# Attention with short convolution on one core: first maxima taken later, bank-freeing products ahead of splits, and load buffers of its own for the last y

## The chip, the core and the metric

The kernel runs on one core of a Trainium2 chip. A core has TensorE (PE: matmuls, with PEld for the loading of their stationary operand), VectorE (DVE), ScalarE (ACT), GpSimd (POOL) and SyncE (SP, which here only issues DMAs). Each engine runs its own list of instructions in order; they wait for one another by semaphores. PE writes only into PSUM, whose banks hold 128 x 512 numbers of 32 bits; DVE and ACT read it out. The metric is the device time of one execution in microseconds (us).

## What is computed

One layer of a diffusion backbone, batch 1, 1024 latent tokens on a grid of 16 x 64, 256 context tokens, model width 1024:

```python
h = rmsnorm(x, norm_g) * (1 + scale[:, None]) + shift[:, None]
hc = rmsnorm(ctx, norm_g) * (1 + scale_c) + shift_c
q, k, v, za, u, bg, cg, zc = jnp.split(h @ w_in, SPLIT_POINTS, axis=-1)
...
attn = neighbourhood_attention(q, k, heads(v), kc, vc, rpb) * jax.nn.silu(za)
conv = gated_short_conv(u, bg, cg, zc, conv_w, conv_b)
x_new = x + gate[:, None] * (jnp.concatenate([attn, conv], axis=-1) @ w_out)
```

The attention has 8 heads of 64. A query sees a window of 8 x 16 latent keys with a learned position bias, and all context keys, in one softmax. The convolution branch is `bg * conv3(cg * u) * silu(zc)` over 512 channels.

## The kernel before

Every product is made of three matmuls: each operand is split into a rounded high part (a cast on ACT) and the rest (a subtraction on DVE), and high x high, high x low and low x high are summed in PSUM (`mm3`). So each block of weights costs a load, a cast and a "split" before PE can use it.

There are three stages. In the first the inputs are normed, and q, k, v are projected and spilled to HBM. The second is the attention, in which all four engines run in an order written out by hand: every instruction is chained behind the one before it on its engine (`strict`). The third is the output projection, where the planner that builds the kernel orders the instructions of each engine itself, by when it believes that their inputs are there.

**The attention** runs over 35 quarters (`quarter(n)`, L1123), one fourth of a head each, as a software pipeline. Quarter n makes the scores of unit n (two key blocks against the queries that see them), the context scores of unit n+1, the exponentials of unit e = n-2, and the products with v of unit o = n-3. Keys lie along partitions, so the maximum over the keys of a query is a maximum over partitions. It goes this way: running maxima are kept in `mx` (DVE, `ctx_max` and `lat_max`); PE turns a block of 128 queries of it into a bank `pmx` (a transpose); DVE reduces it to one column `rm`; PE turns that column back, spread over all partitions; ACT copies it to `mg`, and DVE subtracts `mg` from the scores ahead of the exponential. `turned(e)` gives the blocks that are needed for unit e: one for e = -1 and for the last, two for the others.

Before the change all of this stands at the head of a quarter: turn and reduction first, then the products of the context (`ctx_out`) and waiting DVE work, then the turn back and the copy, then the scores. In quarter 1 (e = -1) and quarter 2 (e = 0) there are no products yet between turn and turn back.

**Filler.** Between the steps of a quarter PE works at 16 "units", the projections of the gates and of the convolution branch: each is a [1024 x 128] slice of `w_in` against h in two halves of 512 tokens, each half in one of two PSUM banks (`pu`, tag "U", L369). One call of `next(fill)` is a tick of six matmuls. `TICKS[n]` says how many ticks quarter n has. The work of the other engines for the filler is put in queues of "chores": `soon` (splits of the next unit's weights, copies, the product `cu`) and `slow` (convolution taps and products `cv`). `do_dves(3)` in a quarter emits up to three DVE chores, `soon` first. A chore with `frees` set (L469) is the product `times(half, ps, True)` of a unit CBG, which reads the unit's bank; the next unit's half may not start before it.

**The output stage** needs y[f] for eight blocks f, in the order 4, 5, 6, 0, 1, 2, 3, 7 (`FORDER`). `put_y` (L1417) loads a half into `tb`, casts it to `yh` on ACT and subtracts on DVE to give `yl`. Blocks 0 to 3 are the pairs of attention heads, 4 to 7 the convolution groups. Pair 3 is finished here: its gate `zs` and its sums `rb` are loaded too. All `tb` and `zs` come from one ring of four buffers (tag "zt"); the loads are issued from ACT's queue. `yh` and `yl` of the last block lie in the pool `rp`, which takes over the space of h once the last unit is through.

Of the kernel before, what the change touches and what calls it, by code (L numbers as in the profile page):

```python
# [10 lines left out]
F32 = mybir.dt.float32  # L11
# [3 lines left out]
ALU = mybir.AluOpType  # L15
AX = mybir.AxisListType
# [3 lines left out]
P = 128  # L20
# [6 lines left out]
NH, HD = 8, 64  # L27
# [2 lines left out]
CTXT = 3  # L30
FORDER = [4, 5, 6, 0, 1, 2, 3, 7]

TICKS = [2, 3, 3, 3, 3, 2, 3, 3, 2] + 2 * (8 * [3] + 2 * [4]) + 3 * [3] + [4, 5, 4]
EPS = 1e-6


# [3 lines left out]
def body(tc, es, x, ctxt, w_ada, b_ada, w_in, q_g, k_g, rpbr, w_out, vecs, cst, out):  # L40
# [21 lines left out]
    pe, act, dve, pool = every = [ordered(e) for e in (nc.tensor, nc.scalar, nc.vector, nc.gpsimd)]  # L62
    sp = ordered(nc.sync)

    def sbuf(name, side=None, bufs=1):
        kw = {} if side is None else {"side": side}
        return tc.tile_pool(name=name, bufs=bufs, reuse_waits="tile", **kw)

    def psum(name):
        return tc.tile_pool(name=name, bufs=1, space=PSUM, reuse_waits="tile")  # L70
# [42 lines left out]
    ident = ci[:, 0:P]  # L113
# [207 lines left out]
    def do_acts():  # L321
        for c in soon + (slow if not any(c[1] and c[1].__name__ == "product" for c in soon) else []):
            if c[0]:
                c[0]()
                c[0] = None

    def do_dves(most=99):
        for queue in chores:
            while queue and not queue[0][0] and (queue is soon or most > 0 and not soon):
                on_dve = queue.pop(0)[1]  # L330
                if on_dve:
                    on_dve()
                    most -= 1
# [45 lines left out]
    def blocked(v):  # L379
        return v.rearrange("p (b r c) -> p b r c", b=2, r=16)  # L380

    def by_row(v):
        return v.rearrange("p (r b c) -> p b r c", r=16, b=2)

    def natural(v, half):
        return v.rearrange("p (r b c) -> p b r c", r=16, b=4)[:, 2 * half:2 * half + 2]
# [136 lines left out]
    def load_sums(f, half, rb, queue):  # L523
        for i in range(2):
            queue.dma_start(rb[64 * i:64 * i + 64],
                            ri_d[f][i:i + 1, half * 512:(half + 1) * 512].broadcast_to([64, 512]))
# [306 lines left out]
    for m in range(1, 4):  # L833
        k, new, last = 2 * m, m < 3, m == 3
# [84 lines left out]
    psm = es.enter_context(psum("psm"))  # L919
# [182 lines left out]
    def pair_of(n):  # L1102

        h, g = divmod(n, 4)
        return [(a, heads[h], 2 * g + a) for a in range(2)] if 0 <= h < NH else []

    def both(v, n, part=slice(0, 31)):

        lo, hi = span(2 * (n % 4))
        return v[:, :, part.start * 12:min(part.stop, hi - lo) * 12]  # L1110

    def maxima_of(n):

        lo, hi = span(2 * (n % 4))
        v = mg[:]
        return bass.AP(v.tensor, v.offset + lo * 16, [list(v.ap)[0], [4, 2], [16, hi - lo], [1, 12]])

    def turned(n):

        g = n % 4  # L1120
        return [b for b, there in (((2 * g + 2) % NB, n + 1 < 4 * NH), (2 * g + 1, n >= 0)) if there][::-1 if g < 3 else 1]

    def quarter(n):  # L1123

        live = lambda m: 0 <= m < 4 * NH
        ticks = TICKS[n]
        e, o = n - 2, n - 3  # L1130
        blocks = turned(e) if -1 <= e < 4 * NH else []
        nb = len(blocks)
        if blocks:
            pm = psm.tile([P, 512], F32, name="pmx", tag="C", bufs=2)
            for i, b in enumerate(blocks):
                pe.transpose(pm[:, i * P:(i + 1) * P], mx[:, b * P:(b + 1) * P], ident)
            rm = ap.tile([P, 2], F32, name="rm", tag="rm", bufs=8)
            dve.tensor_reduce(rm[:, :nb], pm[:, :nb * P].rearrange("p (i k) -> p i k", i=nb), AX.X, ALU.max)
        while lat_rest:
            lat_rest.pop()()  # L1140
        if live(o):
            heads[o // 4].ctx_out(o % 4)
        do_dves(3)
        if gating and next(gating[0], "end"):
            gating.pop(0)
        if blocks:
            for i in range(nb):
                pe.transpose(pm[:, 256 + i * P:256 + (i + 1) * P], rm[:, i:i + 1].broadcast_to([P, P]), ident)
            v, step = mg[:, blocks[0] * P:], (blocks[-1] - blocks[0]) * P or P
            act.copy(bass.AP(v.tensor, v.offset, [list(v.ap)[0], [step, nb], [1, P]]),  # L1150
                     pm[:, 256:256 + nb * P].rearrange("p (i k) -> p i k", i=nb))
        now = pair_of(n)
        for i, hd_, j in now:
            hd_.scores(j, sbank[:, i])
        if n == 0:
            next(fill)
            ticks -= 1
        ctx_now = [m for m in ([0, 1] if n == 0 else [n + 1]) if live(m)]
        for m in ctx_now:
            heads[m // 4].ctx_scores(m % 4)  # L1160
        if live(e):
            ctx_rest = heads[e // 4].ctx_exp(e % 4)
            sb = sbs.pop(e)
            w = both(sb, e)
            w4 = w.rearrange("p a (c r) -> p a c r", r=12)
            dve.tensor_tensor(w4, w4, maxima_of(e), ALU.subtract)
            exps[e] = [ap.tile([P, 2, 384], F32R, name=m, tag=m, bufs=2) for m in ("phl", "pll")]
            ph, pl = (both(v, e) for v in exps[e])
            act.activation(ph, w, AF.Exp)
            act.activation(w, w, AF.Exp)  # L1170
        for _ in range(n > 0):
            next(fill, None)
        done = []
        if o >= 0:
            pho, plo = exps.pop(o)
            for i, hd_, j in pair_of(o):
                hd_.lat_out(j, pho[:, i], plo[:, i])
                if j in (5, 7):
                    done.append((hd_, j // 7))
                    if j == 7 and hd_.s:  # L1180
                        ready.append(hd_.p)
        if now:
            sb = sbs[n] = sb_new()
            bt = now[0][1].bt[:].rearrange("p v n -> p (v n)")[:, :1128].rearrange("p (a n) -> p a n", a=2)
            for at, slot, w_ in (((0, 31, 8), (8, 15, 16)), ((0, 0, 31),), ((0, 0, 31),), ((0, 0, 15), (15, 39, 8)))[n % 4]:
                dve.tensor_tensor(sb[:, :, at * 12:(at + w_) * 12], sbank[:, :, at * 12:(at + w_) * 12],
                                  bt[:, :, slot * 12:(slot + w_) * 12], ALU.add)
            for m in ctx_now:
                heads[m // 4].ctx_max(m % 4)
            for i, hd_, j in now:  # L1190
                hd_.lat_max(j, sb[:, i])
        if live(e):
            ctx_rest()
            lat_rest.append(lambda: dve.tensor_tensor(pl, w, ph.bitcast(F32), ALU.subtract))
            if n + 1 >= len(TICKS) or TICKS[n + 1] == 2:
                lat_rest.pop()()
        for _ in range(ticks - (n > 0)):
            next(fill, None)
        for hd_, bank_ in done:
            hd_.finish(bank_)  # L1200
        do_acts()
# [36 lines left out]
    for n in range(NT + 3):  # L1238


        p, t = divmod(n, NB)
# [122 lines left out]
    with sbuf("att") as ap, psum("psb") as psb:  # L1364
        sbank = psb.tile([P, 2, 512], F32, name="pss")
        strict[:] = every
        mx = ap.tile([P, T], F32, name="mx")
        sb_new = lambda: ap.tile([P, 2, 384], F32, name="sb", tag="sb", bufs=3)
        mg = ap.tile([P, T], F32, name="mg")
        heads[0].load_v()  # L1370
        for n in range(len(TICKS)):
            h, g = divmod(n, 4)
# [7 lines left out]
            if ready:  # L1380
                p = ready.pop()
# [20 lines left out]
    op = es.enter_context(sbuf("op"))  # L1402
# [14 lines left out]
    def put_y(yp, f):  # L1417

        yh = yp.tile([P, T], F32R, name=f"yh{f}")
        yl = yp.tile([P, T], F32R, name=f"yl{f}")  # L1420
        for half in range(2):
            cols = slice(half * 512, (half + 1) * 512)
            tb = op.tile([P, 512], F32, name="tb", tag="zt", bufs=4)
            if f == NPAIR - 1:
                zs = op.tile([P, 512], F32, name="zs", tag="zt", bufs=4)
                rb = op.tile([P, 512], F32, name="rb", tag="rb", bufs=2)
                act.dma_start(zs, z_d[f][:, cols])
                act.dma_start(tb, o_d[f][:, cols])
                load_sums(f, half, rb, pool)
                act.activation(zs, zs, AF.Silu)  # L1430
                dve.tensor_tensor(zs, zs, rb, ALU.mult)
                dve.tensor_tensor(tb, tb, zs, ALU.mult)
            else:
                act.dma_start(tb, y_d[f][:, cols])
            tv = blocked(tb[:]) if f < NPAIR else by_row(tb[:])
            act.copy(natural(yh[:], half), tv)  # L1436
            dve.tensor_tensor(natural(yl[:], half), tv, natural(yh[:].bitcast(F32), half), ALU.subtract)
        y[f] = yh, yl
# [93 lines left out]
```

## Time and profile before

| | us |
|---|---|
| median of 3 runs | 633.08 |
| runs | 632.79 to 636.38 |
| the profiled execution | 633.06 |
| its span, from first to last instruction | 631.3 |
| granted TensorE clock, mean | 1.000 |

Of the span the projections take until about 266 us (the first scores follow), the attention with its filler until about 522, the last convolution unit until 539, and the output projection the rest. Times of instructions in the profile are from the start of the span. In a row of the timeline stand start, length, engine, line, operation, output <- inputs, sizes, and how many instructions were merged; in brackets the idle time of the engine before it and what ended it. Operations that go through the ordering helper all have its line, L55, so they are told apart by their tiles. "ACTq" and "SPq" are DMA issues from the queues of ACT and SP. The columns of a stretch (rows "a:b") are its length, the busy time of PE, PEld, DVE, ACT and POOL, the granted clock, the share of the DMA engines' time and GB/s.

### The profile page before, as it was taken

Reading aid. Unit: us, or ns where it says so; the run is one execution under the profiler, and the core shown is the slowest. Engines: PE = TensorE matmul, PEld = TensorE weight load, DVE = VectorE, ACT = ScalarE, POOL = GpSimd, SP = SyncE. Lnnn points to the kernel's source line nnn. Section 1 sums busy time; section 2 is a strip of 40 time slices with the busy share of each in tenths; the row PEclk is TensorE's granted clock in tenths of the full one; section 3 lists DMA queues with packets and bytes.
Section 4 is the critical chain, followed back from the end, with each engine's and each line's share of the span. In section 5 each row is a group of like instructions: output and inputs, shape, how many; then the busy total and the mean of one; then the engine's idle time right before and its main releaser. Section 6 shows DMA issues by size and latency. Waiting matters only on the chain.

```text
span 631.3 us, 10013 instructions
## 1 busy us (share of the span) xinstructions
PE 622.9 (99%) x3488; PEld 538.6 (85%) x3488; DVE 433.5 (69%) x889; ACT 326.7 (52%) x712; POOL 78.6 (12%) x102
## 2 busy tenths in 40 slices
PE   8999999999999999989999999999999999999998
PEld 3577899999999999878888888888888888878887
DVE  1887857866857755467897778987998865585111
ACT  4776935425626446346576568567774845450000
POOL 1305014123223222000000000000000002004100
PEclk9999999999999999999999999999999999999999
DMA  8983638967875993975475562766542235964521
GB/s 315 363 290 109 179 122 263 280 207 221 273 247 176 293 335 134 338 230 213 135 237 150 181 194 104 239 232 193 171 135 76 60 109 148 359 208 149 197 101 50
DMA packets 104030, 126.45 MB, mean 200 GB/s; under 512 B 10689, under 2 KB 70553, under 8 KB 102700
## 3 DMA queue, kind: packets, MB, share of 16 engines
q1 hardware_dynamic: 97516, 114.24, 54.7%
q10 hardware_dynamic: 6208, 11.05, 5.5%
q0 software_dynamic: 256, 0.54, 0.3%
q8 instruction: 27, 0.44, 0.3%
q14 instruction: 23, 0.19, 0.1%
HBM read 89.04 MB, written 39.04 MB: 203 GB/s over the span
## 4 chain that ended last, share of the span: by engine, by line
PE 89%; DMA 4%; DVE 3%; issue 1%; ACT 1%; POOL 0%; SPq 0%; ACTq 0%; DVEq 0%; POOLq 0%
PE pu L55 27%; PE pacc L55 21%; PE po L55 8%; PE acc L55 6%; PE tr L55 5%; PE cacc L55 4%; PE pout L74 3%; PE pout L76 3%; PE pout L75 3%; PE pss L55 3%; PE pmx L55 2%; PE pc L55 2%; DMA tb<-y_d 2%; DMA woraw<-in_w_out 2%; PE trA L55 1%
## 5 line engine op out<-in xcount | busy, mean ns | idle before, releaser
L55 PE MATMUL pu<-h,uh 128*128 128x512 f32 x544 | 169.7, 393 | 0.9 <-DVE cv L55 0.9
L55 PE MATMUL pacc<-w,h 128*128 128x384 f32 x768 | 138.4, 337 | 0.0
L55 PEld LDWEIGHTS pacc<-w,h 128*128 128x128 f32 x768 | 132.8, 188 | 0.2
L55 PEld LDWEIGHTS pu<-h,uh 128*128 128x128 f32 x544 | 97.6, 188 | 18.0 <-DVE cv L55 1.3
L55 PE MATMUL pu<-h,ul 128*128 128x512 f32 x272 | 106.5, 392 | 0.0
L55 PEld LDWEIGHTS pu<-h,ul 128*128 128x128 f32 x272 | 51.1, 188 | 11.1
L55 POOL TENSOR_TENSOR ss<-ss,few 128x4 f32<-128x4 f32 (+1 forms) x40 | 42.0, 1050 | 124.7 <-DVE ss L55 124.7
L74 PE MATMUL pout<-woh,yh 128*128 128x512 f32 (+2 forms) x136 | 51.6, 380 | 0.3 <-ACT yh L1436 0.3
L75 PE MATMUL pout<-wol,yh 128*128 128x512 f32 (+2 forms) x136 | 51.6, 379 | 0.0
L76 PE MATMUL pout<-woh,yl 128*128 128x512 f32 (+2 forms) x136 | 50.8, 379 | 0.0
L55 PE MATMUL acc<-h,w 128*128 128x512 f32 x144 | 38.1, 404 | 0.8 <-ACT h L55 0.8
L55 ACT ACTIVATE sq<-pacc 128x256 f32<-128x256 f32 x32 | 12.4, 387 | 48.2 <-PE pacc L55 44.3
L55 DVE TENSOR_REDUCE rm<-pmx 128x2 f32<-128x256 f32 (+1 forms) x33 | 13.7, 416 | 33.8 <-PE pmx L55 33.7
L55 ACT COPY mg<-pmx 128x256 f32<-128x256 f32 (+1 forms) x33 | 12.1, 366 | 47.1 <-PE pmx L55 37.7
L55 DVE TENSOR_TENSOR mx<-mx,sb 128x372 f32<-128x372 f32 (+2 forms) x64 | 31.8, 498 | 2.0
L55 PE MATMUL po<-phl,v 128*65 128x276 f32 (+2 forms) x192 | 32.0, 269 | 0.0
L55 ACT ACTIVATE qn<-pacc,ss 128x64 f32<-128x64 f32 x128 | 30.2, 332 | 3.0 <-POOL ss L55 3.0
L55 DVE TENSOR_REDUCE ss<-sq 128x4 f32<-128x260 f32 (+1 forms) x40 | 15.6, 391 | 22.9 <-ACT sq L55 22.9
L55 PEld LDWEIGHTS acc<-h,w 128*128 128x128 f32 x144 | 25.5, 188 | 6.5 <-ACT h L55 1.2
L1462 DVE TENSOR_TENSOR ot<-pout,xr 128x512 f32<-128x512 f32 (+2 forms) x9 | 5.7, 632 | 36.5 <-PE pout L76 36.5
L74 PEld LDWEIGHTS pout<-woh,yh 128*128 128x128 f32 x136 | 25.6, 188 | 5.4 <-ACT yh L1436 0.7
L76 PEld LDWEIGHTS pout<-woh,yl 128*128 128x128 f32 x136 | 25.6, 188 | 4.7
(159 smaller groups left out, 1188.8 us busy)
## 6 DMA issues: line engine op xcount, KB each, us to landing
uraw<-in_w_in SPq DMA_DIRECT2D x34, 256.0 KB
q_d<-qs SPq DMA_DIRECT2D x32, 256.0 KB
k_s<-k_d SPq DMA_DIRECT2D x8, 1024.0 KB
q_s<-q_d SPq DMA_DIRECT2D x16, 512.0 KB
wr<-in_w_in SPq DMA_DIRECT2D x40, 192.0 KB
slab<-in_w_ada SPq DMA_DIRECT2D x6, 1024.0 KB
v_d<-vs SPq DMA_DIRECT2D x20, 260.0 KB
v<-v_d SPq DMA_DIRECT2D x16, 325.0 KB
```

The lines of the kernel that those rows point to most:

```text
L55: i = emit(*a, **kw)
L74: i = pe.matmul(ps, ah, bh, start=first, stop=False)
L75: pe.matmul(ps, ah, bl, start=False, stop=False)
L76: pe.matmul(ps, al, bh, start=False, stop=last)
L1462: dve.tensor_tensor(ot[:, c], ps[c.start][:, c], xr[:, c], ALU.add)
```

## The change

Four edits. (1) The maxima become a function in two steps. For e = -1 the turn and reduction move from the head of quarter 1 to behind its scores, its maxima on DVE and its first tick, and the turn back with its copy to behind the quarter's other ticks. For e = 0 the turn stays at the head of quarter 2, and the turn back moves behind the scores and context scores. From e = 1 on nothing moves. (2) `do_dves` first takes a chore that frees a bank, if one stands at the head of `slow`. (3) The last three quarters have 5, 4, 4 ticks instead of 4, 5, 4. (4) The loads of the last y get two buffers in its own pool.

```diff
-TICKS = [2, 3, 3, 3, 3, 2, 3, 3, 2] + 2 * (8 * [3] + 2 * [4]) + 3 * [3] + [4, 5, 4]
+TICKS = [2, 3, 3, 3, 3, 2, 3, 3, 2] + 2 * (8 * [3] + 2 * [4]) + 3 * [3] + [5, 4, 4]
...
     def do_dves(most=99):
+        while most > 0 and slow and slow[0][2] is not None and not slow[0][0]:
+            slow.pop(0)[1]()
+            most -= 1
         for queue in chores:
...
+    def maxima(e):
+
+        blocks = turned(e) if e < 4 * NH else []
+        nb = len(blocks)
+        if not blocks:
+            return None
+        pm = psm.tile([P, 512], F32, name="pmx", tag="C", bufs=2)
+        for i, b in enumerate(blocks):
+            pe.transpose(pm[:, i * P:(i + 1) * P], mx[:, b * P:(b + 1) * P], ident)
+        rm = ap.tile([P, 2], F32, name="rm", tag="rm", bufs=8)
+        dve.tensor_reduce(rm[:, :nb], pm[:, :nb * P].rearrange("p (i k) -> p i k", i=nb), AX.X, ALU.max)
+
+        def back():
+            for i in range(nb):
+                pe.transpose(pm[:, 256 + i * P:256 + (i + 1) * P], rm[:, i:i + 1].broadcast_to([P, P]), ident)
+            v, step = mg[:, blocks[0] * P:], (blocks[-1] - blocks[0]) * P or P
+            act.copy(bass.AP(v.tensor, v.offset, [list(v.ap)[0], [step, nb], [1, P]]),
+                     pm[:, 256:256 + nb * P].rearrange("p (i k) -> p i k", i=nb))
+        return back
...
     def quarter(n):
...
+        back = maxima(e) if e >= 0 else None
...
+        if back and n > 2:
+            back()
         now = pair_of(n)
         for i, hd_, j in now:
             hd_.scores(j, sbank[:, i])
...
             heads[m // 4].ctx_scores(m % 4)
+        if back and n == 2:
+            back()
         if live(e):
...
             for i, hd_, j in now:
                 hd_.lat_max(j, sb[:, i])
+        back = maxima(-1) if n == 1 else None
         if live(e):
...
         for _ in range(ticks - (n > 0)):
             next(fill, None)
+        if back:
+            back()
         for hd_, bank_ in done:
...
-            tb = op.tile([P, 512], F32, name="tb", tag="zt", bufs=4)
+            tb = yp.tile([P, 512], F32, name="tb", tag="zt", bufs=4 if yp is op else 2)
```

The lines taken out of `quarter` (turn, reduction, turn back and copy at its head) are those of the new function.

More of the change, by code (lines that the diff above doesn't have):

```diff
@@ L1130, in quarter @@
         e, o = n - 2, n - 3
[L1131 to L1138, printed above, removed]
+        back = maxima(e) if e >= 0 else None
         while lat_rest:
@@ L1145, in quarter @@
             gating.pop(0)
[L1146 to L1151, printed above, removed]
+        if back and n > 2:
+            back()
         now = pair_of(n)
```

## The prediction

> **What bounds the kernel now.** I read the page first, then the list of waits of TensorE, then the timeline around each of those waits.
>
> ```profile
> span 631.3 us, 10013 instructions
> ## 1 busy us (share of the span) xinstructions
> PE 622.9 (99%) x3488; PEld 538.6 (85%) x3488; DVE 433.5 (69%) x889; ACT 326.7 (52%) x712; POOL 78.6 (12%) x102
> ```
>
> TensorE (PE) is busy 99% of the span, and the change neither adds nor drops a matmul. So a gain can only come out of the time in which PE stands still, and a loss only out of new standstills. These are two of PE's waits that the change aims at (total, times, longest); a third, on `mx`, and one at the end stand in the timelines further down:
>
> ```profile
> PE pu L55 <- DVE cv L55: 0.9, 2, 0.5
> PE pmx L55 <- DVE rm L55: 0.9, 2, 0.5
> ```
>
> A wait costs more than its idle time, because the ends of matmuls are modelled and overlap the next start. I therefore measure by starts. The chain of waits has stretches without a gap that give the steady steps (start, length, instructions):
>
> ```profile
> 274.47 4.09 PE pu L55 x18
> ...
> 482.51 1.63 PE pu L55 x6
> ...
> 509.97 0.11 PE pmx L55
> ```
>
> A filler matmul of 512 columns takes 4.09/18 = 0.227 us; a "tick" of filler (six of them) is 1.36, three ticks are 4.09. A turn (`pmx`, one block) takes 0.11.
>
> **The first maxima (1.5 us gained).** PE at the start of the attention, quarters 1 and 2 (start, length, instruction):
>
> ```profile
> 271.08 0.39 PE L55 MATMUL pu<-h,ul 128*128 128x512 f32 x1
> 272.31 0.30 PE L55 MATMUL pmx<-ci,mx 128*128 128x128 f32 x1 [0.84 <-DVE mx L55]
> 272.99 0.32 PE L55 MATMUL pmx<-ci,rm 128*128 128x128 f32 x1 [0.38 <-DVE rm L55]
> 273.07 0.93 PE L55 MATMUL pss<-q_s,k_s 128*128 128x372 f32 x4
> 273.83 0.63 PE L55 MATMUL pc<-q_s,kc_s 128*128 128x256 f32 x4
> ...
> 278.40 0.38 PE L55 MATMUL pmx<-ci,mx 128*128 128x128 f32 x2
> 279.29 0.43 PE L55 MATMUL pmx<-ci,rm 128*128 128x128 f32 x2 [0.52 <-DVE rm L55]
> ```
>
> The last filler matmul starts at 271.08 and leaves PE free at 271.31; the turn of the maxima starts at 272.31: 1.00 lost. The turn back could start 0.11 later, at 272.42, and starts at 272.99: 0.57 lost. In quarter 2 two turns take 0.22, and the turn back starts 0.89 after the first of them: 0.67 lost. Together 2.24 us.
>
> With the change quarter 1 goes straight to the scores (273.07 to 273.83: 0.76), the context scores (from 273.83 to three ticks before quarter 2's start at 278.40, that is 274.31: 0.48) and a tick. Then come the turn, two ticks and the turn back. Scores start at 271.31, so the turn is due at 271.31 + 0.76 + 0.48 + 1.36 = 273.91, and the turn back 0.11 + 2.73 later, at 276.75. Nothing may be late there:
>
> ```profile
> 271.21 0.95 DVE L55 TENSOR_TENSOR mx<-mx,sb 128x288 f32<-128x288 f32 x2
> ...
> 275.58 1.12 DVE L55 TENSOR_TENSOR mx<-mx,sb 128x372 f32<-128x372 f32 x2
> ...
> 280.17 0.69 DVE L55 TENSOR_TENSOR sc<-sc,mg 128x512 f32<-128x512 f32 x1 [0.33 <-ACT mg L55]
> ...
> 282.74 1.13 DVE L55 TENSOR_TENSOR mx<-mx,sb 128x372 f32<-128x372 f32 x2
> ```
>
> The first quarter's maxima are done at 271.21 + 0.95 = 272.16, well before 273.91. The second quarter's end 3.63 after its scores begin (273.07 to 276.70), so at 274.94. The reduction stands behind them on VectorE (DVE) and has until 276.75. Both stalls of quarter 1 are hidden.
>
> Quarter 2 then begins at 276.86 and puts scores and context scores (1.24) between the turn (0.22) and the turn back, which falls at 278.32. The reduction's round trip of 0.89 ends at 277.75, so this stall is hidden too. The transposes and context scores share a ring of two banks, whose order shifts by one: quarter 2's context scores now take the bank of quarter 1's maxima, read by an mg copy from 277.22 on (below), 0.6 before they start at 277.84. So no wait there, though with little to spare. But the move has a price: the copy of the maxima on ScalarE (ACT) now stands behind another one.
>
> ```profile
> 279.76 0.38 ACT L55 COPY mg<-pmx 128x256 f32<-128x256 f32 x1 [1.90 <-PE pmx L55]
> 280.92 0.59 ACT L55 COPY sc<-pc 128x512 f32<-128x512 f32 x1 [0.78 <-PE pc L55]
> ```
>
> Today mg is copied first, 0.47 after the turn back starts (279.29 to 279.76), and sc 0.65 after the context scores start (279.29 + 0.22 + 0.76 = 280.27 to 280.92). In the change sc stands first: context scores start at 276.86 + 0.22 + 0.76 = 277.84, so sc is copied from 278.49 to 279.08, and mg behind it until about 279.4. Ahead of both stand quarter 1's own mg copy, from 276.75 + 0.47 = 277.22, and the split and the filler's copy that used to run before it. By the 0.59 of sc these end near 278.5, just in time. The subtraction `sc<-sc,mg`, 0.03 behind mg's end today, starts at 279.43, and from it to the end of the maxima is 280.17 to 283.87 = 3.70, which gives 283.13. PE, after the turn back (0.22) and three ticks, wants these maxima for quarter 3 at 278.32 + 0.22 + 4.09 = 282.63. With the 0.15 that the first stall shows between DVE's end (272.16) and PE's start (272.31), quarter 3 starts at 283.28: a new stall of 0.65. By the same steps it starts today at 279.29 + 0.22 + 1.24 + 4.09 = 284.84. The gain is 1.56, and I book 1.5. Its bounds are 2.2, if the new stall does not appear, and 0.3 (rival B).
>
> **Products first (1.2 us gained).** One of the two places:
>
> ```profile
> 403.74 0.68 DVE L55 TENSOR_TENSOR ul<-uraw,uh 128x512 fp32r<-128x512 f32 x1
> 404.34 1.28 DVE L55 TENSOR_TENSOR cv<-pu,cv 128x512 f32<-128x512 f32 x2
> ```
>
> ```profile
> 405.08 0.73 PE L55 MATMUL pu<-h,uh 128*128 128x512 f32 x2 [0.45 <-DVE cv L55]
> ```
>
> PE cannot begin the next unit before the first product has read the bank. The product stands behind the split `ul`. With the change it starts where the split started, 0.60 earlier, so PE starts at 404.48 instead of 405.08. Its idle time there is 0.45, and with the 0.15 of hand-over from above 0.60 is what there is to win: all of it. The second place is the unit that starts at 482.51 in the chain above: its tick takes 1.63 there, and the list has 0.5 as the longest of the two waits; I give it the same 0.6. The split now runs behind both products, 1.28 later. It holds the second half of the next unit's weights, which PE needs two ticks into that unit (2.7 us), so it costs nothing; without that cover it would cost at most 0.68. Bounds: 0 (something else in front of the product) to 1.25.
>
> **The last y (0.2 gained).**
>
> ```profile
> 568.32 0.50 PE L74 MATMUL pout<-woh,yh 128*128 128x512 f32 x1 [0.31 <-ACT yh L1436]
> ```
>
> ```profile
> 566.61 0.62 ACT L1436 CAST yh<-tb 128x512 fp32r<-128x512 f32 x1 [0.96 <-DMA tb<-y_d]
> ...
> 567.66 0.61 ACT L1436 CAST yh<-tb 128x512 fp32r<-128x512 f32 x1
> ```
>
> ```profile
> 566.06 0.68 DVE L1432 TENSOR_TENSOR tb<-tb,zs 128x512 f32<-128x512 f32 x1
> ```
>
> PE idles 0.31 here, with the hand-over of 0.15 some 0.46 is lost: it was due at 567.86. It starts 0.05 after a cast that ends at 568.27. That cast is of pair 3, whose product is done at 566.74. It came late because ACT sat 0.96 us waiting for a load of the last y, which itself had waited for a buffer of the shared ring. With buffers of its own the load is no longer held, and the cast of pair 3 may start at 566.74, ending 567.36, before 567.86. That is worth 0.46. But the order on ACT is the planner's in this stage, and the two loads now move into an earlier stretch:
>
> ```profile
> 540.00:550.00 10.00, 10.00 (x46) 8.28 (x45) 5.88 (x10) 5.01 (x9) 0.00 (x0) 1.00 1.02 341
> ```
>
> There the DMA engines are full (share 1.02, 341 GB/s). The two loads are 2 x 128 x 512 x 4 B = 0.52 MB, 1.54 us at that rate, by which the other y loads can be late. So the bounds are 0.46 gained and 1.5 lost; I take 0.2 gained, nearer to the row that shows the wait. The Trainium skill says in "Trainium Kernel Development and Optimization", Key Constraints, that DMAs issued from SP, ACT and POOL queues all run on the same 16 engines and interleave, which speaks against this part; the row with 1.02 agrees that they are full. "DMA: Bandwidth & Descriptors", Where 436 GB/s comes from, gives about 358 GB/s for HBM traffic of one core; an estimate from that page would be 1.46 us instead; the row's 341 lies a little under it.
>
> **Ticks.** The last three quarters have 5, 4, 4 ticks instead of 4, 5, 4: the same 13, and the last quarter begins at the same place. Only the second one starts a tick later.
>
> ```profile
> 510.12 0.29 DVE L55 TENSOR_REDUCE rm<-pmx 128x1 f32<-128x128 f32 x1 [2.53 <-PE pmx L55]
> ```
>
> DVE stands idle for 2.53 us ahead of it, so the tick moves into an idle engine, and I cost it at nothing. Without that cover it would cost 1.36.
>
> **Sum.** The profiled execution took 633.06 us (span 631.3); the median of the three runs is 633.08, so the two can be read as one. 1.5 + 1.2 + 0.2 = 2.9; 633.06 - 2.9 = 630.2.
>
> **The rivals.**
> B, half the gain: PE's turn in quarter 1 waits for the second quarter's maxima too (274.94 + 0.15 = 275.09 instead of 273.91), if the wait is put on the whole of `mx` and not on its first block. Everything to quarter 3 moves by 1.18, and of 1.56 only 0.38 stays; 633.06 - 0.38 - 1.2 - 0.2 = 631.3. If instead the product is not at the head of its queue when it matters, 1.2 goes, and the time is 631.4. For it: such waits are put in by the framework. Against: block 0 is columns 0 to 127, and the second pair writes from 144 on.
> D, all gained: neither the 0.65 of quarter 3 nor any loss at the end. 633.06 - 2.24 - 1.2 - 0.46 = 629.2.
> C, slower: the last y's second load is put on ACT's queue ahead of pair 2's loads, while its data are still on the way to HBM.
>
> ```profile
> 547.33 1.95 ACTq L1434 DMA_DIRECT2D tb<-y_d  x2
> ...
> 551.98 0.62 ACT L1436 CAST yh<-tb 128x512 fp32r<-128x512 f32 x1 [2.04 <-DMA y_d<-cv]
> ```
>
> The store `y_d<-cv` is named as landing just before 551.98. If ACT's queue waits for it in front of the issue at 547.33, the issues behind it come up to 4.6 us later; pair 3 takes its buffers from these, so its cast at 568.3 and PE with it move by as much. 633.06 - 1.5 - 1.2 + 4.6 = 635.0. It makes the kernel slower as soon as the queue is held for over 2.7 us. For it: DMA is full there. Against: the planner sees the store and has kept PE in work up to that 0.46.
>
> **How the numbers follow.** Forecast 0.60 (own range 629.6 to 630.8); B 0.15; D 0.10; C 0.10; 0.05 for what I do not see. The range goes from 628.6 (D less 0.6, twice the 0.29 by which the lowest run lies under the median) to 633.2 (the end where C makes it no faster), which leaves out most of C and the unseen. One per cent, about what a measurement of this kernel can tell from no change, is 6.3 us. No sum of stalls here reaches that: faster 0.02. C would have to hold ACT for over 9 us: slower 0.03; within 0.95.
>
> **What would show it.** In the profile after: PE's waits no longer name `cv`, and `rm` no longer; scores of quarter 1 begin where the filler ends, near 271.3; `mx` shows one wait of some 0.5 in quarter 3. Then 564 to 570 has no PE wait on `yh`. Wrong would be a wait of `pout` in 550 to 570, or the first `pmx` at 275.1.

## The result and the profile after

| | us |
|---|---|
| before, median of the 7 runs beside it | 633.08 (631.9 to 636.38) |
| after, median of 7 runs | 629.81 (628.79 to 630.4) |
| after / before | 0.9941, 95% interval 0.9921 to 0.996 |
| the profiled execution after | 630.4, span 628.6, clock 0.999 |

The change makes the kernel 3.27 us faster by the medians, half a per cent; 2.9 had been forecast (630.2). In the last set of experiments below, on another chip, the same two kernels gave 629.92 and 633.69, ratio 0.9942 (0.993 to 0.9955).

The head of the page after, and the line of the chain of waits with its shares by engine:

```profile
span 628.6 us, 10005 instructions
...
PE 621.7 (99%) x3487; PEld 538.5 (86%) x3488; DVE 433.5 (69%) x889; ACT 326.5 (52%) x712; POOL 77.6 (12%) x102
...
PE 96%; DMA 2%; SPq 1%; ACT 0%; issue 0%; DVE 0%; ACTq 0%
```

The same line of the chain before:

```profile
PE 89%; DMA 4%; DVE 3%; issue 1%; ACT 1%; POOL 0%; SPq 0%; ACTq 0%; DVEq 0%; POOLq 0%
```

PE's busy time is within 1.2 us of what it was; the chain now hardly leaves PE. The list of PE's waits after (total, times, longest):

```profile
PE acc L55 <- POOL c L55: 1.4, 1, 1.4
PE acc L55 <- ACT h L55: 0.8, 1, 0.8
PE tr L55 <- DVE xx L55: 0.5, 1, 0.5
PE tr L55 <- DVE ab L55: 0.5, 1, 0.5
PE pmx L55 <- ACT uh L55: 0.4, 1, 0.4
PE tr L55 <- DVE rw L55: 0.3, 1, 0.3
PE acc L55 <- issue: 0.2, 1, 0.2
```

The waits on `cv`, on `rm` and on `yh` are gone. `acc` and `tr` belong to the head of the program, before the attention, and differ from one execution to the next. Behind that head one wait is new: `pmx`, 0.4, which the page puts down to `uh`. It is the stall at quarter 3 that the prediction had worked out. PE in quarters 1 to 3 after (start, length, instruction):

```profile
272.05 0.84 PE L55 MATMUL pss<-q_s,k_s 128*128 128x372 f32 x4
...
274.58 0.27 PE L55 MATMUL pmx<-ci,mx 128*128 128x128 f32 x1
...
277.43 0.27 PE L55 MATMUL pmx<-ci,rm 128*128 128x128 f32 x1
277.53 0.38 PE L55 MATMUL pmx<-ci,mx 128*128 128x128 f32 x2
...
278.91 0.38 PE L55 MATMUL pmx<-ci,rm 128*128 128x128 f32 x2
...
283.05 0.39 PE L55 MATMUL pu<-h,ul 128*128 128x512 f32 x1
283.84 0.41 PE L55 MATMUL pmx<-ci,mx 128*128 128x128 f32 x2 [0.41 <-ACT uh L55]
```

Neither the turn of quarter 1 (274.58) nor the turns back (277.43, 278.91) have idle time ahead of them any more. Quarter 3 is where PE stands: its last filler matmul starts at 283.05 and a step takes 0.23, so 283.84 is 0.56 late (0.57 with unrounded times). What VectorE and ScalarE did before it:

```profile
274.48 1.12 DVE L55 TENSOR_TENSOR mx<-mx,sb 128x372 f32<-128x372 f32 x2
...
280.00 0.69 DVE L55 TENSOR_TENSOR sc<-sc,mg 128x512 f32<-128x512 f32 x1 [0.76 <-ACT mg L55]
...
282.57 1.13 DVE L55 TENSOR_TENSOR mx<-mx,sb 128x372 f32<-128x372 f32 x2
```

```profile
279.11 0.59 ACT L55 COPY sc<-pc 128x512 f32<-128x512 f32 x1
279.59 0.38 ACT L55 COPY mg<-pmx 128x256 f32<-128x256 f32 x1
...
283.23 0.60 ACT L55 CAST uh<-uraw 128x512 fp32r<-128x512 f32 x1
```

This is the order that the prediction followed: `sc` ahead of `mg` on ACT, DVE idle 0.76 for `mg`, the maxima done at 282.57 + 1.13 = 283.70, and PE 0.14 behind them. The page's `uh` is only the last of several signals: it ends at 283.83, 0.01 before PE, while PE starts 0.05 behind a cast of ACT that it really waits for (568.27 to 568.32 in the prediction's rows) and 0.15 behind an operation of DVE (272.16 to 272.31).

The first of the two places with a product, where PE had waited for `cv`:

```profile
402.91 1.28 DVE L55 TENSOR_TENSOR cv<-pu,cv 128x512 f32<-128x512 f32 x2
...
403.17 0.63 PE L55 MATMUL pc<-q_s,kc_s 128*128 128x256 f32 x4
...
403.65 0.73 PE L55 MATMUL pu<-h,uh 128*128 128x512 f32 x2
...
404.11 0.69 DVE L55 TENSOR_TENSOR ul<-uraw,uh 128x512 fp32r<-128x512 f32 x1
```

`cv` now runs ahead of `ul`, and the filler follows the context scores without idle time. In the output stage ACT looks like this, where the last y now has its own buffers:

```profile
541.82 0.33 ACTq L1451 DMA_DIRECT2D tb<-y_d  x1
...
548.18 1.67 ACT L1430 CAST woh<-woraw 128x512 fp32r<-128x512 f32 x3 [5.38 <-DMA tb<-y_d]
...
551.74 0.44 ACTq L1451 DMA_DIRECT2D tb<-y_d  x1
```

The two loads of the last y are the issues at 541.82 and 551.74; before they were at 563.77 and 566.78. ACT's longest idle time there has grown from 3.04 to 5.38 us, but nothing on PE waits for it.

The cast of pair 3 for which PE waited before has not come earlier. It is the one at 565.82 here, 39.27 us behind ACT's last `zs<-pu` (526.55); before, it was 39.05 behind it (567.66 and 528.61). What has changed is PE's own list:

```profile
565.82 0.62 ACT L1453 CAST yh<-tb 128x512 fp32r<-128x512 f32 x1
```

```profile
565.79 0.39 PE L74 MATMUL pout<-woh,yh 128*128 128x512 f32 x1
566.02 0.39 PE L75 MATMUL pout<-wol,yh 128*128 128x512 f32 x1
566.24 0.39 PE L76 MATMUL pout<-woh,yl 128*128 128x512 f32 x1
...
567.15 0.39 PE L74 MATMUL pout<-woh,yh 128*128 128x512 f32 x1
567.38 0.39 PE L75 MATMUL pout<-wol,yh 128*128 128x512 f32 x1
567.60 0.39 PE L74 MATMUL pout<-woh,yh 128*128 128x512 f32 x1
```

Pair 3 is known by its rows: L74 and L75 take turns there, and its products with `yl` (L76) come later. They start with the 127th output matmul before (568.32) and with the 133rd here (567.15). The six matmuls from 565.79 to 567.15 belong to the second half of the output's columns (y[4] and y[5]); with the own buffers the planner puts them ahead of pair 3. The cast ends at 566.44, 0.65 behind the start of the 127th matmul and 0.71 ahead of the 133rd, so the six cover it.

**How the profiles are compared.** When the attention's first score starts differs from one execution to the next by itself: 266.97 before, 267.71 after, 266.17 to 268.01 over the thirteen profiles of this study, though the program up to there is the same in all of them. So I measure from that first score and subtract the same landmark before. "Quarter 3" is its first turn, "last product" the last matmul of the attention, "127th" the 127th output matmul, which waited at 568.32 before, "end" the end of the span. The last column is what PE lost at that output matmul: from the start of the matmul before it, less a step of 0.23. In the seven kernels with the shared ring the 127th is the first of pair 3; in the six with own buffers it is the first of the six matmuls put ahead, and pair 3's first, the 133rd, starts without a wait in all six too.

| kernel | first score | quarter 3 | last product | 127th | end | lost there |
|---|---|---|---|---|---|---|
| before | 266.97 | 0 | 0 | 0 | 0 | 0.47 |
| after | 267.71 | -1.71 | -2.81 | -3.28 | -3.41 | 0 |
| e1 maxima alone | 266.21 | -1.71 | -1.57 | -0.24 | -0.19 | 1.31 |
| e2 products alone | 268.01 | +0.03 | -1.06 | -1.23 | -1.21 | 0.30 |
| e3 last y alone | 267.40 | +0.05 | +0.28 | -0.12 | -0.24 | 0 |
| e4 ticks alone | 266.17 | +0.03 | +0.08 | +0.69 | +0.72 | 1.08 |
| e5 turn back first | 266.38 | -2.27 | -3.45 | -3.42 | -3.54 | 0 (0.46 at 552) |
| e6 split doubled | 266.29 | 0.00 | +1.53 | +1.80 | +1.81 | 0.74 |
| e7 shared ring | 267.05 | -1.71 | -2.86 | -3.02 | -3.00 | 0.31 |
| a1 changed again | 267.31 | -1.72 | -2.84 | -3.31 | -3.44 | 0 |
| a2 shared ring again | 266.96 | -1.71 | -2.81 | -1.95 | -1.92 | 1.21 |
| a3 last y alone again | 266.78 | +0.06 | +0.01 | -0.29 | -0.42 | 0 |
| a4 turns and tick mended | 266.93 | -2.25 | -3.75 | -4.12 | -4.24 | 0 |

### The profile page after: what moved, and what is told of

It is laid out like the page before. It is cut to its first block, busy times and chain, and to the rows that moved or that the text cites. A ratio compares the mean times of both kernels' runs of the same rounds, so it can differ in the third digit from the quotient of the medians.

```text
span 628.6 us, 10005 instructions
## 1 busy us (share of the span) xinstructions
PE 621.7 (99%) x3487; PEld 538.5 (86%) x3488; DVE 433.5 (69%) x889; ACT 326.5 (52%) x712; POOL 77.6 (12%) x102
## 4 chain that ended last, share of the span: by engine, by line
PE 96%; DMA 2%; SPq 1%; ACT 0%; issue 0%; DVE 0%; ACTq 0%
PE pu L55 29%; PE pacc L55 21%; PE po L55 8%; PE acc L55 6%; PE pout L75 5%; PE pout L74 5%; PE pout L76 5%; PE tr L55 4%; PE cacc L55 4%; PE pss L55 3%; PE pc L55 2%; PE pmx L55 2%; DMA xx<-in_x 2%; PE trA L55 1%; PE trB L55 1%; SPq L55 1%
## 5 line engine op out<-in xcount | busy, mean ns | idle before, releaser
L75 PE MATMUL pout<-wol,yh 128*128 128x512 f32 (+2 forms) x136 | 51.6, 379 | 0.0
L74 PE MATMUL pout<-woh,yh 128*128 128x512 f32 (+2 forms) x136 | 51.5, 379 | 0.0
L76 PE MATMUL pout<-woh,yl 128*128 128x512 f32 (+2 forms) x136 | 50.8, 379 | 0.0
L55 ACT COPY sc<-pc 128x512 f32<-128x512 f32 x32 | 18.8, 589 | 21.1 <-PE pc L55 21.0
L74 PEld LDWEIGHTS pout<-woh,yh 128*128 128x128 f32 x136 | 25.6, 188 | 4.7
```

Of the source, the lines that this page charges most:

```text
L55: i = emit(*a, **kw)
L74: i = pe.matmul(ps, ah, bh, start=first, stop=False)
L75: pe.matmul(ps, ah, bl, start=False, stop=False)
L76: pe.matmul(ps, al, bh, start=False, stop=last)
```

## The experiments

**e1, the first maxima alone.** The kernel before with edit (1) and nothing else:

```diff
-        blocks = turned(e) if -1 <= e < 4 * NH else []
...
+        back = maxima(e) if e >= 0 else None
...
+        if back and n > 2:
+            back()
...
+        if back and n == 2:
+            back()
...
+        back = maxima(-1) if n == 1 else None
...
+        if back:
+            back()
```

> Only the first maxima moved. Theory (the parts add up, each wins back the standstill that its row shows): measured from the first score, quarter 3 begins 1.7 us earlier than before (2.24 won, 0.57 given back at the turn of quarter 3), the two waits on cv stay (the last product of the attention is 1.6 to 1.7 earlier), the wait of 0.3 on yh at the end stays. Span from the first score on 1.6 to 1.8 shorter. Rival (the gains need one another): DVE, which then gets its work earlier, lets PE wait later on; under 1.0 is left at the last product.

Measured: quarter 3 stands 1.71 ahead, and 1.57 of that is left at the end of the attention. Yet the span is only 0.19 shorter (time 632.15). The list of waits of this kernel says where it went:

```profile
PE pout L74 <- ACT yh L1450: 1.2, 1, 1.2
```

Most of the attention's gain was given back in the output stage: PE lost 1.31 instead of 0.47 at the 127th output matmul, and 0.46 in four steps around 553, where a cast of `yh` came late.

**e2, the products first, alone.**

```diff
     def do_dves(most=99):
+        while most > 0 and slow and slow[0][2] is not None and not slow[0][0]:
+            slow.pop(0)[1]()
+            most -= 1
```

> Only the bank-freeing products taken first. Theory: quarters 1 to 19 as before to 0.1 us, then 0.6 earlier after each of the two places, 1.2 earlier at the last product of the attention; no PE wait on cv is left. Rival: the split that now comes later lets the next unit wait; under 0.8 in all, and a PE wait on ul appears.

Measured: no wait on `cv`; by the quarters' landmarks the kernel gains 0.61 between quarters 19 and 20 and has gained 0.59 more at quarter 30. The last product is 1.06 ahead and the end 1.21 (time 632.91). The product was the price at both places.

**e3, own buffers for the last y, alone.**

```diff
-            tb = op.tile([P, 512], F32, name="tb", tag="zt", bufs=4)
+            tb = yp.tile([P, 512], F32, name="tb", tag="zt", bufs=4 if yp is op else 2)
```

> Only the own buffers for the last y. Theory: the same as before up to the output stage, then 0.5 to 0.6 earlier from the 127th output matmul on, and no PE wait on yh. Rival (the earlier loads crowd the full DMA engines, and the planner's order does not fit them): a new PE wait in the output stage, nothing gained or up to 1.5 lost.

Measured: the wait on `yh` is gone and no other comes in its place. From the last product to the end the kernel gains 0.28 + 0.24 = 0.52 (time 633.27), as expected; from the first score only 0.24 is left. The attention in front of it drifted by 0.28 in small steps, of which the repeat a3 keeps 0.01. This edit alone gives PE and ACT the order of the changed kernel in the output stage, with the six matmuls ahead of pair 3. The cast of pair 3 starts 39.64 behind ACT's last `zs`, later than the 39.05 before.

**e4, the ticks alone.**

```diff
-TICKS = [2, 3, 3, 3, 3, 2, 3, 3, 2] + 2 * (8 * [3] + 2 * [4]) + 3 * [3] + [4, 5, 4]
+TICKS = [2, 3, 3, 3, 3, 2, 3, 3, 2] + 2 * (8 * [3] + 2 * [4]) + 3 * [3] + [5, 4, 4]
```

> Only the ticks 5, 4, 4. Theory: quarter 33 begins 1.36 later than before, the last product of the attention and everything behind it at the same time to 0.1 us. Rival: a PE wait in the last three quarters goes or comes, 0.3 us or more at the last product.

Measured: the second of the three quarters starts 1.46 later, the last product 0.08: the tick costs nothing in the attention, as booked. But the end is 0.72 later (time 632.99), 0.61 of it at the 127th output matmul, where PE lost 1.08. The instructions of the output stage are the same as before, in the same order, and PE arrives at the same time. So what PE loses there varies from one execution to the next.

These four were timed once each, and the single time of the kernel before beside them was 636.06, near the top of its scatter (631.9 to 636.72 in all), so I judge them by the landmarks.

**e5, the turn back ahead of the context scores.** The first of a second set, against the new stall at quarter 3:

```diff
+        if back and n == 2:
+            back()
         for m in ctx_now:
             heads[m // 4].ctx_scores(m % 4)
-        if back and n == 2:
-            back()
```

> The changed kernel, except that quarter 2's turn back is put ahead of its context scores, so that the copy of the maxima (mg) stands ahead of the copy sc on ACT. Measured from the first score, the changed kernel stood 1.71 ahead of the kernel before at quarter 3 and lost 0.57 there. Theory (the order of the two copies on ACT makes that stall; the reduction's round trip of 0.89 is still covered by three score matmuls, 0.76, but for some 0.1): quarter 3 starts 2.1 to 2.3 ahead of the kernel before, its loss falls from 0.57 to 0.15 or less, and the span from the first score is 0.4 to 0.6 shorter than the changed kernel's, if nothing later takes it back. Rival (DVE's own queue is what is late, whatever the order on ACT): quarter 3 stays at 1.6 to 1.8 ahead, with its loss of 0.5 to 0.6.

Measured: quarter 3 is 2.27 ahead instead of 1.71, and nothing is lost there. The timeline of this kernel around it:

```profile
277.57 0.38 ACT L55 COPY mg<-pmx 128x256 f32<-128x256 f32 x1
...
277.98 0.69 DVE L55 TENSOR_TENSOR sc<-sc,mg 128x512 f32<-128x512 f32 x1
278.05 0.59 ACT L55 COPY sc<-pc 128x512 f32<-128x512 f32 x1
...
280.55 1.13 DVE L55 TENSOR_TENSOR mx<-mx,sb 128x372 f32<-128x372 f32 x2
...
281.95 0.38 PE L55 MATMUL pmx<-ci,mx 128*128 128x128 f32 x2
```

`mg` is copied ahead of `sc`, DVE starts 0.03 behind its end without idle time, and the maxima end at 281.68, 0.27 before PE wants them. The order of two copies on ACT was the whole of that stall. The end, however, is only 0.13 ahead of the changed kernel's: 0.46 were lost in four steps around 552, where a cast of `yh` came late for PE (time 628.97, one run). e1 shows the same four steps without this edit.

**e6, the split done twice.** The kernel before, with the suspected price raised:

```diff
-            dve.tensor_tensor(wl, raw, wh[:].bitcast(F32), ALU.subtract)
+            for _ in range(2 if slow and slow[0][2] == 0 else 1):
+                dve.tensor_tensor(wl, raw, wh[:].bitcast(F32), ALU.subtract)
```

> The kernel before, with the split ul done twice on DVE (the second time with the same result) where a product that frees a unit's bank is behind it, that is at the two places where PE waits for cv. Theory (PE waits there for the product, and the split ahead of it is the whole of the price of 0.60 each): each of the two waits grows by one split of 0.6 to 0.7, the list of waits shows cv with 2.0 to 2.4 in all instead of 0.9, and the last product of the attention comes 1.2 to 1.4 later than in the kernel before, from the first score. Rival (the split is only beside the path, and something else, such as the copy of pu by ACT, ends the wait): cv stays at 0.9 and the last product within 0.3.

Measured, in the list of PE's waits:

```profile
PE pu L55 <- DVE cv L55: 2.4, 2, 1.2
```

From 0.9 to 2.4 for one more split at each of two places, and the last product 1.53 later (time 634.2, one run), a little more than expected. The split ahead of the product stands on PE's path with its whole length.

**e7, the changed kernel with the shared ring.** It undoes edit (4) alone. By then I thought that with the shared ring loads set the pace of the last y, so that a PE that arrives earlier only waits longer, and that the own buffers protect what the attention gains.

```diff
-            tb = yp.tile([P, 512], F32, name="tb", tag="zt", bufs=4 if yp is op else 2)
+            tb = op.tile([P, 512], F32, name="tb", tag="zt", bufs=4)
```

> The changed kernel without own load buffers for the last y (its loads go through the shared ring of four as in the kernel before); all else as changed. Theory (with the shared ring the casts of the last pairs are paced by loads, which land when they land, so PE arrives earlier and waits): the last product of the attention is 2.7 to 2.9 ahead of the kernel before from the first score, as in the changed kernel, but PE then waits for yh 1.0 to 2.5 in all, and the span from the first score is only 0.5 to 1.8 shorter than before; time 631.2 to 632.6, some 1.5 to 2.8 over the changed kernel. Rival (the waits on yh that the single parts showed are scatter from one execution to the next, and own buffers are worth the 0.2 to 0.5 that they gave alone): wait on yh 0.1 to 0.6, span 2.4 to 2.8 shorter than before, time 630.0 to 630.5.

Measured: time 631.51 (629.47 to 632.48 in 10 runs) against 633.39 (13 runs), ratio 0.9962 (0.9947 to 0.9978). That is within the theory's range. But its profile is not: PE, 2.86 early, loses 0.31 at the last y, less than the kernel before with a PE on time, and the span is 3.00 shorter, more than either side expected. The profiled execution (630.15) is one of the shortest of the ten. So four kernels were timed again on one more chip.

**a1 and a2, the changed kernel with own buffers and with the shared ring, side by side.** The kernels are those of the change and of e7.

> The changed kernel again, beside the three others on one chip, to price the last y's own buffers with and without the attention's two edits. Theory (with the shared ring, loads and not PE set the pace of the last y, so own buffers give more when PE arrives 2.8 earlier): 1.0 to 2.0 faster than the changed kernel with the shared ring. Rival (the two parts simply add): 0.3 to 0.8 faster than it, as much as own buffers gain in the kernel before.

> The changed kernel with the shared ring for the last y, again. Theory: 1.3 to 2.2 faster than the kernel before, of the 2.8 that its attention gains; its runs scatter over 2 us or more, more than those of the changed kernel. Rival (the parts add): 2.5 to 3.0 faster than the kernel before, with no more scatter than the changed kernel.

Measured: 629.92 (629.32 to 630.87) with own buffers, 630.02 (629.67 to 631.63) with the shared ring, 5 runs each; 633.69 before (15 runs). The difference is 0.1 by the medians and 0.5 by the means (630.00 and 630.47): not the theory's 1.0 to 2.0, and at most the rival's 0.3 to 0.8. Against the kernel before, the shared ring is 3.67 faster by the medians, above both expected ranges, and its runs spread over 1.96, the others over 1.55. Here the profile of the shared ring shows the large loss, 1.21, with PE just as early as in e7. The two profiles of one kernel show what differs. ACT in e7:

```profile
525.83 0.60 ACT L55 ACTIVATE zs<-pu 128x512 f32<-128x512 f32 x1 [1.83 <-PE pu L55]
...
532.66 0.62 ACT L1453 CAST yh<-tb 128x512 fp32r<-128x512 f32 x1 [1.58 <-DMA tb<-y_d]
...
541.85 1.14 ACT L1430 CAST woh<-woraw 128x512 fp32r<-128x512 f32 x2 [0.28 <-DVE yl L1454]
...
563.66 0.62 ACT L1453 CAST yh<-tb 128x512 fp32r<-128x512 f32 x1 [1.03 <-DMA tb<-y_d]
```

and in a2:

```profile
525.80 0.60 ACT L55 ACTIVATE zs<-pu 128x512 f32<-128x512 f32 x1 [1.83 <-PE pu L55]
...
533.36 0.62 ACT L1453 CAST yh<-tb 128x512 fp32r<-128x512 f32 x1 [2.02 <-DMA tb<-y_d]
...
543.06 1.14 ACT L1430 CAST woh<-woraw 128x512 fp32r<-128x512 f32 x2 [0.63 <-DVE yl L1454]
...
564.65 0.62 ACT L1453 CAST yh<-tb 128x512 fp32r<-128x512 f32 x1 [0.89 <-DMA tb<-y_d]
```

Both start the stage at 525.8. Then ACT waits for loads; at 533 a2 is 0.70 behind, at 543 1.21, and it carries 0.99 of that to the last casts. Stretches of the two, e7 first (length, busy time of PE, PEld, DVE, ACT, POOL, granted clock, DMA share, GB/s):

```profile
536.00:542.00 6.00, 6.00 (x28) 4.95 (x28) 5.10 (x9) 4.11 (x8) 0.00 (x0) 1.00 1.04 379
```

```profile
536.00:542.00 6.00, 6.00 (x28) 4.96 (x27) 4.61 (x8) 3.83 (x8) 0.00 (x0) 1.00 1.00 346
```

The DMA engines are full in both, but they move 379 GB/s in one and 346 in the other. So between these two executions of one kernel, what PE loses at the 127th goes with how soon the loads land, at the same arrival of PE. The seven profiles with the shared ring say the same. Over the 22 us from ACT's last `zs<-pu` on, e7, e2, e6, the kernel before, e4, a2 and e1 moved 322, 320, 312, 311, 307, 297 and 294 GB/s, and PE lost 0.31, 0.30, 0.74, 0.47, 1.08, 1.21 and 1.31: but for two pairs of neighbours, the slower the loads, the larger the loss. That is a correlation: no run sets the rate by itself.

With that my theory falls: were the loads a fixed pace, PE in e7 would have lost 0.47 + 2.86, over 3 us. The traces show why they are not. ACT's last `zs` comes 7.15 us behind the last product of the attention in all thirteen profiles, and all but the first load of the stage's y are issued behind it. So the loads start earlier when PE arrives earlier.

**a3, own buffers alone again**, as in e3.

> The kernel before with own buffers for the last y alone, again. Both theories: 0.2 to 0.8 faster than the kernel before (its one profile showed 0.53 in the output stage). Under the theory that the parts need each other this is clearly less than own buffers are worth in the changed kernel; under the rival it is the same.

Measured: 632.52 (632.02 to 634.5, 11 runs) against 633.69, 1.17 faster by the medians and 0.67 by the means; the ratio is 0.999 (0.9979 to 1.0), so the times alone hardly tell it from no gain. In its profile the end gains 0.42 + 0.01 from the last product on, again without a wait on `yh`.

**a4, a version to beat the change.** e5, quarter 1's turn back a tick earlier, and the ticks moved so that one more lies ahead of the turn of quarter 32, where PE lost 0.26 in the changed kernel:

```diff
-TICKS = [2, 3, 3, 3, 3, 2, 3, 3, 2] + 2 * (8 * [3] + 2 * [4]) + 3 * [3] + [5, 4, 4]
+TICKS = [2, 3, 3, 3, 3, 2, 3, 3, 2] + 2 * (8 * [3] + 2 * [4]) + [3, 3, 4] + [4, 4, 4]
...
+        if back and n == 2:
+            back()
         for m in ctx_now:
             heads[m // 4].ctx_scores(m % 4)
-        if back and n == 2:
-            back()
...
-        for _ in range(ticks - (n > 0)):
+        for i in range(ticks - (n > 0)):
             next(fill, None)
-        if back:
-            back()
+            if back and i == 0:
+                back()
```

> A version meant to beat the changed kernel: quarter 2's turn back ahead of its context scores, quarter 1's turn back a tick earlier (both, so that the copies of the maxima stand early on ACT), and the last six quarters' ticks as 3, 3, 4, 4, 4, 4 so that the tick more comes before the turn where PE lost 0.26 (quarter 32). All else as changed. Theory (what is left in the attention is these two stalls, 0.57 and 0.26): the last product of the attention 0.7 to 0.9 ahead of the changed kernel from the first score, no wait on mx, time 0.3 to 0.9 below the changed kernel, the rest given back at the last y. Rival (the output stage is paced by its loads with own buffers too, so all of it is given back): the attention gains the same, time within 0.2 of the changed kernel.

Measured: 628.92 (628.04 to 629.54), 1.0 below the changed kernel on the same chip; ratio to before 0.9927 (0.9913 to 0.994). The time gained is a little over the theory's 0.3 to 0.9. The last product is 3.75 - 2.84 = 0.91 ahead of a1's, the end 0.80. Quarter 3 is 2.25 ahead, as in e5 (2.27), so the earlier turn back of quarter 1 adds nothing that shows; another 0.3 came between quarter 31 and the last product. In its list of PE's waits only `acc` and `tr` are left, 2.6 us in all, and they lie before the attention. This is the fastest of the kernels here that were timed more than once.

## Why the prediction was right, and where it was off

**The first maxima** (booked 1.5, worked out 1.56). Both stalls of quarter 1 and that of quarter 2 went, and the new one came where it had been placed. Quarter 2 started 0.67 later in the profile than the prediction's 276.86, as its first score did (0.75). Taking that off, `sc` starts at 278.44 (278.49 predicted), DVE's subtraction at 279.33 (279.43), the maxima end at 283.03 (283.13), and PE is late by 0.57 (0.65). The gain is 1.71 at quarter 3, and 1.57 at the end of the attention in e1. e5 showed that the order on ACT is the cause: turned round, the stall is gone. That the stall could be foreseen came from listing what each moved step stands behind on its engine, not from PE's own rows.

**The products first** (booked 1.2). In the changed kernel 0.60 are gained between quarters 19 and 20, and 0.58 between 29 and 30, where 0.60 each was predicted; e2 shows the same alone, and e6 the reverse. The split behind the product cost nothing.

**The ticks** (booked 0): e4 agrees.

**The last y** (booked 0.2). Here the number was too small, and the step behind it was wrong. The prediction had the loads no longer held, the cast of pair 3 therefore 0.91 earlier (567.36 instead of 568.27), and PE on time. The loads did move (541.82), and ACT no longer waits for one ahead of that cast. But the cast came 0.22 later behind ACT's last `zs` than before (39.27 and 39.05), and 39.27 to 40.01 behind it in the six profiles with own buffers, against 38.88 to 40.37 in the seven with the shared ring. In the changed kernel the product that it reads now ends on DVE (565.11 + 0.68 = 565.79) only 0.03 ahead of it, where before it ended 0.92 ahead (566.74 and 567.66). Had PE alone kept its order, it would by these rows have lost about 0.70 (an estimate: 566.44 and a hand-over of 0.05, less 565.79). What took the loss away are the six matmuls that the planner put ahead of pair 3: in all six profiles the cast ends 0.41 to 0.71 before PE needs it. The prediction named the order on ACT as the planner's, and did not ask what becomes of PE's. So that this part gained at all is luck as far as its argument goes.

The size is a draw as well. The rows had given a loss of 0.46 here, and I took less than half of it. The seven profiles with the shared ring lost 0.30 to 1.31, on average 5.42 / 7 = 0.77, so the 0.46 was one draw from a wide scatter, and below their mean. Of the six with own buffers five show no step of PE from the last product on that is more than 0.11 too long, and e5 shows 0.46 around 552. After a wait there is a bit more: in a2 the row of PE and its neighbours are

```profile
564.92 0.39 PE L76 MATMUL pout<-woh,yl 128*128 128x512 f32 x1
566.36 0.50 PE L74 MATMUL pout<-woh,yh 128*128 128x512 f32 x1 [1.05 <-ACT yh L1453]
566.70 0.40 PE L75 MATMUL pout<-wol,yh 128*128 128x512 f32 x1
566.93 0.40 PE L74 MATMUL pout<-woh,yh 128*128 128x512 f32 x1
```

From 564.92 to 566.36 are 1.44, a loss of 1.21 where the page shows 1.05 idle; the next step takes 0.34 instead of 0.23, another 0.11. These rows also show the order with the shared ring, pair 3 right behind the 126th. Between the changed kernel and the one before, the output stage is 3.41 - 2.81 = 0.60 shorter: 0.47 and this rest of 0.13. The Trainium skill says in "Trainium Kernel Development and Optimization", Key Constraints, that DMAs from the queues of SP, ACT and POOL share 16 engines and interleave; the shares of 1.00 to 1.04 above agree with it. I had read it as speaking against this part, but it says nothing of the order in which PE's matmuls stand, and that order took the wait away.

**The sum.** By landmarks: 1.57 + 0.60 + 0.58 + 0.60 = 3.35, against 2.9; the span from the first score is 3.41 shorter. By the span itself it is 2.66, since this execution's first score came 0.75 later. Of the 0.45 over the booked sum, 0.40 are the last y's. The medians of the two chips give 3.27 and 3.77. The forecast's own range, 629.6 to 630.8, held the time.

**The rivals.** B fell: the turn of quarter 1 started at 274.58, ahead of the end of the second quarter's maxima at 274.48 + 1.12 = 275.60. It waited for its block alone. D's first half fell, the stall at quarter 3 came; its second half, no loss at the last y, came about, but by PE's order. C fell: ACT was held longer by the loads, but PE had work throughout.

**What stays open.** What own buffers are worth in the time, with an early PE: 0.1 by the medians on one chip; at the end of the profiles 0.41 (after and e7) and 1.52 (a1 and a2). Whether PE's new order would do as much with the shared ring: no run has the one without the other. e7's runs on its chip were 1.88 faster than before, and a2's on the other 3.67, the same kernel. And what sets the rate of the loads, 346 or 379 GB/s in the same stretch of one program, no run here tells.

## What to carry to other kernels

When a step is moved, write down for each engine what it now stands behind: a copy of 0.59 us ahead of another one on ACT made, by way of DVE, a new stall of 0.57 on PE, and turning the two round removed it. A product that frees a bank belongs ahead of work that is only needed later: a second split of 0.7 in front of it cost PE 0.7. Before sizing a wait on a load, look for how far it scatters between executions, since one profile shows one draw. Where a planner orders the instructions, compare the order of every engine before and after: an edit to buffers moved six matmuls on PE, and these, not the earlier loads, took the wait away. And compare profiles from a landmark behind the parts that scatter by themselves.

## What the runs showed of the hardware

- Idle time understates a wait of PE on a stationary operand: 1.05 idle was 1.21 from start to start, and 0.11 more in the step after it.
- With DMA share at 1.00 or over, the rate differed by a tenth between two executions of one kernel (346 and 379 GB/s from 536 to 542), and ACT's casts stood 1.21 us apart just behind that stretch.
- The start of the attention, after the same instructions, scattered over 1.84 us (266.17 to 268.01), more than half of what the change gained.
